# A hybrid RG-LRU / gMLP / conv-FFN block on one core: residual steps, one modulation and the last residual are moved

## The chip, the core and the metric

The kernel runs on one core of one Trainium2 chip. The metric is the device time of one execution in microseconds; the table below gives the median of three runs. One execution more was profiled: its trace is what the rows below are read from.

Engines are named as in the profile: PE (TensorE, matmuls), PEld (its weight loads), DVE (VectorE), ACT (ScalarE), POOL (GpSimd), SP (SyncE, which here only issues DMAs).

## The reference

One residual block, 2048 positions, width 1024, one batch element, all float32. What matters here:

```python
mod = silu(c) @ w_ada + b_ada                 # six vectors of 1024: sh_m, sc_m, gt_m, sh_f, sc_f, gt_f
h = rmsnorm(x, g_mix_pre) * (1 + sc_m) + sh_m
y = mixer(h @ w_in) @ w_out                   # RG-LRU heads and gMLP heads, each normed
x = x + gt_m * rmsnorm(y, g_mix_post)         # first residual
h = rmsnorm(x, g_ffn_pre) * (1 + sc_f) + sh_f
up = causal_conv3(h @ w_up)                   # 6144 columns: g_ff, v_ff
y = (gelu(g_ff) * v_ff) @ w_down              # 3072 -> 1024
x = x + gt_f * rmsnorm(y, g_ffn_post)         # last residual
```

## The kernel before, in words

Activations lie with the 1024 channels on partitions (8 blocks of 128) and positions along the free axis. Every matmul is done as three: each float32 operand is split into a high and a low part of the `fp32r` type (`split`, lines 136 and 141), and high x high, high x low and low x high are added in PSUM (`mm3`).

The mixer runs over four chunks of 512 positions (`c` = 0 to 3), the FFN over two chunks of 1024 (`C` = 0, 1). For each FFN chunk an *up* phase runs over 24 blocks of 128 gate and 128 value columns (`f`), and writes the gated product to `gd` in DRAM; then two *down* phases (`t` = 0, 1, 512 positions each) read it back. So the program is: mixer, up 0, down 00, down 01, up 1, down 10, down 11. In an up phase one block (`up_pair`) is seven products of 12 matmuls, 84 in all, made from seven weight pieces (`up_weights`), of which POOL computes four differences (lines 951 to 959), ACT and DVE the split.

Work beside the main line is written as Python generators that stand in a list `bg`; each `tick()` lets every generator go one step. `up_phase` has two ticks a block. Two such generators start at block `PLAIN + 1` = 3 of up 0:

- `late_chunks`: the first residual of mixer chunks 2 and 3, whose mixer outputs were kept in DRAM (`o2d`). One step of `late_post` (line 571 on) loads a tile of `x` and one of `o2d`, does two `scalar_tensor_tensor` (line 583), an add (line 584), a store to `x2d` (line 585), a square on ACT (line 215) and a sum of squares on POOL (line 219). Each chunk has four such steps, then a sum over partitions by two matmuls with a matrix of ones (line 199).
- `ada_task(5, 1)`: the sixth modulation vector, `gt_f`: eight loads of a weight tile and eight multiply-adds (lines 275 and 277), then eight PE transposes (line 284) and two reductions (line 285). The vectors 2, 3 and 4 are made the same way during the mixer (`ada_task(2, 2)`, `(3, 1)`, `(4, 1)`), where each half of the transposes has a PSUM tile of its own, out of four.

The loads of `x` and of the modulation's weights, and POOL's temporary `wt` of line 951, share one SBUF pool of three buffers (`lp`, tag `ld`).

A down phase ends with `evict`: for each of eight PSUM banks ACT squares (line 1074) and copies (line 1075); DVE adds the squares in pairs of blocks (line 1077) and folds the two halves (line 1101). `final()` then makes the norm (lines 199 to 203), scales each block (line 1112), adds a tile of `x2d` loaded into an `ld` buffer (lines 1109 and 1113) and stores the result (line 1114). For down 11 this stands at the end of the program.

The framework's scheduler sets the order of instructions on each engine from the order written, priorities and its own model of durations; an engine works through its queue in that order.

Of the kernel before, what the change touches and what calls it, by code (L numbers as in the profile page):

```python
# [15 lines left out]
P = 128  # L16
# [24 lines left out]
def block_kernel(ctx: ExitStack, tc: tile.TileContext, xt, cols, rows, wada, wada_r, win_k, win_s, win_v, wgate, wsp, wout, wup, wdown, out):  # L41
# [225 lines left out]
    def ada_task(m, pause=0):  # L267

        acc = tp.tile([P, 8, P], F32, tag="t4", name=f"ada_m{m}")
        flat = acc.rearrange("p k c -> p (k c)")  # L270
        for kt in range(8):
            w = lp.tile([P, 8 * P], F32, tag="ld", name=f"wada_{m}_{kt}")
            sync.dma_start(out=w, in_=wada_r[m - 2, kt])
            if kt == 0:
                vec.tensor_scalar(out=flat, in0=w, scalar1=cact[:, 0:1], scalar2=None, op0=ALU.mult)
            else:
                vec.scalar_tensor_tensor(out=flat, in0=w, scalar=cact[:, kt:kt + 1], in1=flat, op0=ALU.mult, op1=ALU.add)
            yield from wait(1 + pause)
        yield from wait(5)
        o = modv[:, m]  # L280
        for q in range(2):
            pt = bank(f"adaps_m{m}_{q}").rearrange("p (b c) -> p b c", c=P)
            for kb in range(4):
                pe.transpose(out=pt[:, kb], in_=acc[:, 4 * q + kb], identity=ident)
            vec.tensor_reduce(out=o[:, 4 * q:4 * q + 4], in_=pt, axis=mybir.AxisListType.X, op=ALU.add)
        vec.tensor_tensor(out=o, in0=o, in1=bav[:, m], op=ALU.add)
# [626 lines left out]
    def conv(C, blk, R):  # L913
# [3 lines left out]
        for t, s in ((1, 1), (0, 2)):  # L917
            vec.scalar_tensor_tensor(out=a[:, s:], in0=R[:, :FT - s], scalar=w[t], in1=a[:, s:], op0=ALU.mult, op1=ALU.add)  # L918
        if C == 0:
            vec.tensor_copy(out=ftails[:, blk], in_=R[:, FT - 2:FT])  # L920
        else:
            for t, s in ((1, 1), (0, 2)):
                vec.scalar_tensor_tensor(out=a[:, :s], in0=ftails[:, blk, 2 - s:], scalar=w[t], in1=a[:, :s], op0=ALU.mult, op1=ALU.add)  # L923
# [104 lines left out]
    def up_phase(C, f0, on=lambda f: None):  # L1028
        before = None
        for f in range(f0, NF):  # L1030
# [2 lines left out]
            next(g)  # L1033
            if before:
                drain(before)
            tick()
            next(g)
            before = g
            tick()
# [4 lines left out]
    def down(C, t):  # L1044
# [21 lines left out]
            mm3(pts[d], (wh[:, d], wl[:, d]), G[f], f == 0, f == NF - 1)  # L1066

        O, acc = [], []

        def evict(d):  # L1070
            if d % 2 == 0:
                acc.append(t4(f"fs{n}_{d}"))
                O.append(t4(f"fo{n}_{d}"))
            act.activation(out=acc[-1][:, d % 2], in_=pts[d], func=AF.Square)
            act.copy(out=O[-1][:, d % 2], in_=pts[d])
            if d % 2 and d > 1:
                vec.tensor_tensor(out=acc[0], in0=acc[0], in1=acc[-1], op=ALU.add)

        for f in range(2):
# [15 lines left out]
        for d in range(8):  # L1095
# [1 line left out]
                mm(f, d)  # L1097
            evict(d)
            tick()
        a = acc[0]  # L1100
        vec.tensor_tensor(out=a[:, 0], in0=a[:, 0], in1=a[:, 1], op=ALU.add)
        hl = rms_split(a[:, 0], f"fr{n}")

        def final():
            r = rms_bcast(hl, 1.0, f"fr{n}")
            yield
            for j in range(4):
                xr = lp.tile([P, 2, 512], F32, tag="ld", name=f"fx{n}_{j}")
                sync.dma_start(out=xr, in_=x2d[C, :, 2 * j:2 * j + 2, sl])
                for b in range(2):  # L1110
                    o = O[j][:, b]
                    vec.scalar_tensor_tensor(out=o, in0=o, scalar=gf[:, 2 * j + b:2 * j + b + 1], in1=r, op0=ALU.mult, op1=ALU.mult)
                vec.tensor_tensor(out=O[j], in0=O[j], in1=xr, op=ALU.add)
                sync.dma_start(out=out[C, :, 2 * j:2 * j + 2, sl], in_=O[j])
                yield
# [27 lines left out]
            tick()  # L1143
        up_plain(0, f)
    drain(*st)
    up_phase(0, PLAIN, lambda f: start(late_chunks(), ada_task(5, 1)) if f == PLAIN + 1 else None)
    drain()
    vec.tensor_tensor(out=gf, in0=modc[:, 40:48], in1=colr("g_ffn_post", 0, 8), op=ALU.mult)
    for t in range(2):
        start(h2_sums(1, t, from_x2(1, t), True))  # L1150
        down(0, t)
        drain()
    up_phase(1, 0, lambda f: [drain(done.pop(0)) for _ in done[:]] if f == 1 else None)
    for t in range(2):
        down(1, t)
# [72 lines left out]
```

## Time and profile before

| | us |
|---|---|
| median of 3 runs | 2222.09 |
| lowest, highest | 2219.21, 2222.97 |
| the profiled execution | 2222.2 |
| its span in the trace | 2220.4 |

| engine | busy us | share of the span |
|---|---|---|
| PE | 2072.0 | 93% |
| PEld | 1700.7 | 77% |
| DVE | 1435.9 | 65% |
| ACT | 928.8 | 42% |
| POOL | 424.8 | 19% |

Matmuls overlap, so a busy PE does not say at what pace it works. A stretch is better judged by the number of matmuls in it and by the granted clock (1.00 is the level of 2.4 GHz, 0.50 that of 1.2 GHz). In the trace, the mixer lies before 674 us, up 0 ends at about 1190, down 00 at 1324, down 01 at 1456, up 1 at 1924, the last matmul of down 11 starts at 2190.89, and the span ends at 2220.4.

### The profile page before, as it was taken

To read this page: it belongs to the slowest core of one execution; us is meant where nothing else is said; L and a number is where in the kernel's file an instruction comes from. 1 tells how busy PE (TensorE), PEld (TensorE's weight loads), DVE (VectorE), ACT (ScalarE), POOL (GpSimd) and SP (SyncE) were. 2 spreads that over 40 slices of the span, in tenths; PEclk is the share of its full clock that TensorE was granted. 3 is DMA by queue.
4 is the path that set the end of the run, shared out by engine and by line. 5 is a ranking of instruction groups with operands and counts; after the bars stand their busy time and mean duration, and the time that the engine had idled before them with its cause. 6 is when DMAs were issued, how large, how long until landed. Compare 5 with 4: busy or idle time off the path is not lost.

```text
span 2220.4 us, 24098 instructions
## 1 busy us (share of the span) xinstructions
PE 2072.0 (93%) x9032; PEld 1700.7 (77%) x9032; DVE 1435.9 (65%) x1598; ACT 928.8 (42%) x1154; POOL 424.8 (19%) x248
## 2 busy tenths in 40 slices
PE   5898969999998998799999999989999999999995
PEld 4686858888877876588888888868888888888883
DVE  7788789795766887898777437474444444533634
ACT  3472733534635544355555344343233332422422
POOL 4454243234203332443320000020000000000000
PEclk9999989999999999899999999999999999999997
DMA  8587568587674887877775546537666666444541
GB/s 315 187 311 286 193 242 291 206 287 256 225 268 164 305 314 265 311 264 276 271 291 189 181 134 215 173 120 286 220 221 224 220 223 221 145 159 149 212 148 60
DMA packets 157748, 501.14 MB, mean 226 GB/s; under 512 B 15296, under 2 KB 15424, under 8 KB 157632
## 3 DMA queue, kind: packets, MB, share of 16 engines
q1 hardware_dynamic: 149568, 470.25, 59.9%
q0 software_dynamic: 6912, 25.17, 2.9%
q10 hardware_dynamic: 1152, 4.19, 0.5%
q8 instruction: 71, 1.16, 0.2%
q14 instruction: 45, 0.37, 0.1%
HBM read 343.31 MB, written 156.24 MB: 225 GB/s over the span
## 4 chain that ended last, share of the span: by engine, by line
PE 73%; DVE 14%; ACT 4%; DMA 4%; issue 4%; POOL 1%; SPq 0%; DVEq 0%; ACTq 0%; POOLq 0%
PE dn L177 8%; PE dn L178 8%; PE dn L179 8%; PE upa L973 7%; PE upa L972 7%; PE upa L971 7%; PE upc L973 3%; PE upc L972 3%; PE upc L971 3%; PE upb L973 2%; PE upb L971 2%; PE upb L972 2%; PE lg L177 1%; PE lg L178 1%; PE lg L179 1%
## 5 line engine op out<-in xcount | busy, mean ns | idle before, releaser
L177 PE MATMUL dn<-gh,wd_h 128*128 128x512 f32 x768 | 297.0, 390 | 2.9 <-ACT fr_r L202 1.6
L178 PE MATMUL dn<-gl,wd_h 128*128 128x512 f32 x768 | 296.6, 389 | 0.0
L141 DVE TENSOR_TENSOR wd_l<-wd_r,wd_h 128x1024 fp32r<-128x1024 f32 x96 | 118.0, 1230 | 231.9 <-ACT wd_h L136 216.1
L179 PE MATMUL dn<-gh,wd_l 128*128 128x512 f32 x768 | 265.0, 389 | 0.0
L136 ACT CAST wd_h<-wd_r 128x1024 fp32r<-128x1024 f32 x96 | 101.2, 1056 | 286.8 <-PE dn L178 276.1
L918 DVE SCALAR_TENSOR_TENSOR a<-Rg,prm,a 128x1023 f32<-128x1023 f32 x92 | 132.4, 1439 | 126.9 <-ACT a L916 126.7
L177 PEld LDWEIGHTS dn<-gh,wd_h 128*128 128x128 f32 x768 | 144.2, 188 | 35.4 <-ACT wd_h L136 3.0
L179 PEld LDWEIGHTS dn<-gh,wd_l 128*128 128x128 f32 x768 | 144.1, 188 | 29.8
L178 PEld LDWEIGHTS dn<-gl,wd_h 128*128 128x128 f32 x768 | 144.2, 188 | 29.8
L918 DVE SCALAR_TENSOR_TENSOR a<-Rv,prm,a 128x1023 f32<-128x1023 f32 x92 | 121.9, 1325 | 38.7 <-ACT a L916 38.5
L951 POOL TENSOR_TENSOR wt<-wuv,wug 128x512 f32<-128x512 f32 x24 | 39.3, 1637 | 523.7 <-DMA wuv<-in_wup_dram 411.7
L916 ACT ACTIVATE a<-Rv,prm 128x1024 f32<-128x1024 f32 x46 | 57.2, 1244 | 133.3 <-DVE Rv L1020 132.6
L136 ACT CAST wt<-wt 128x512 fp32r<-128x512 f32 x72 | 44.7, 622 | 113.3 <-PE upa L973 39.5
L141 DVE TENSOR_TENSOR wt<-wt,wt 128x512 fp32r<-128x512 f32 x72 | 62.7, 873 | 24.0 <-ACT wt L136 23.8
L976 ACT ACTIVATE a<-a 128x1024 f32<-128x1024 f32 x48 | 50.9, 1061 | 53.7 <-DVE a L923 31.9
L1020 DVE TENSOR_TENSOR Rv<-upa,m 128x512 f32<-128x512 f32 x46 | 31.6, 687 | 58.3 <-PE upa L973 58.3
L141 DVE TENSOR_TENSOR gl<-gr,gh 128x1024 fp32r<-128x1024 f32 x48 | 58.5, 1218 | 12.5 <-PE upa L973 6.3
L977 DVE TENSOR_TENSOR a<-a,a 128x1024 f32<-128x1024 f32 x48 | 58.8, 1225 | 2.5 <-ACT a L976 2.5
L916 ACT ACTIVATE a<-Rg,prm 128x1024 f32<-128x1024 f32 x46 | 57.2, 1243 | 4.4 <-DVE a L918 3.2
L136 ACT CAST gh<-gr 128x1024 fp32r<-128x1024 f32 x48 | 50.8, 1058 | 13.3 <-DMA gr<-gd 6.1
L1024 ACT COPY Rg<-upa 128x512 f32<-128x512 f32 x46 | 26.8, 584 | 69.7 <-PE upa L973 69.7
L959 POOL TENSOR_TENSOR wt<-wug,wt 128x512 f32<-128x512 f32 x24 | 39.9, 1662 | 82.4 <-DVE wt L141 55.5
(583 smaller groups left out, 5738.5 us busy)
## 6 DMA issues: line engine op xcount, KB each, us to landing
wd_r<-in_wdown_dram SPq DMA_DIRECT2D x96, 512.0 KB, 4.4
wkd<-wt SPq DMA_DIRECT2D x88, 512.0 KB, 4.0
wkd<-w SPq DMA_DIRECT2D x66, 512.0 KB, 3.7
w<-wkd SPq DMA_DIRECT2D x66, 512.0 KB, 4.3
gd<-a SPq DMA_DIRECT2D x48, 512.0 KB, 3.9
gr<-gd SPq DMA_DIRECT2D x48, 512.0 KB, 3.5
wrt<-wkd SPq DMA_DIRECT2D x44, 512.0 KB, 4.3
wt<-wkd SPq DMA_DIRECT2D x44, 512.0 KB, 4.6
```

The costliest lines, as they stand in the source:

```text
L136: act.copy(out=hi, in_=src)
L141: (leng or vec).tensor_tensor(out=lo, in0=src, in1=hi.bitcast(F32), op=ALU.subtract)
L177: pe.matmul(out=out, lhsT=wh, rhs=mh, start=first, stop=False)
L178: pe.matmul(out=out, lhsT=wh, rhs=ml, start=False, stop=False)
L179: pe.matmul(out=out, lhsT=wl, rhs=mh, start=False, stop=last)
L916: act.activation(out=a, in_=R, func=AF.Identity, scale=w[2], bias=col("ffn_conv_b", blk))
L918: vec.scalar_tensor_tensor(out=a[:, s:], in0=R[:, :FT - s], scalar=w[t], in1=a[:, s:], op0=ALU.mult, op1=ALU.add)
L971: pe.matmul(out=pt, lhsT=wh, rhs=mh, start=first and not more and k == 0, stop=False, skip_group_check=more)
L972: pe.matmul(out=pt, lhsT=wh, rhs=ml, start=False, stop=False, skip_group_check=more)
L973: pe.matmul(out=pt, lhsT=wl, rhs=mh, start=False, stop=last and k == 3, skip_group_check=more)
L976: act.activation(out=g, in_=g, func=AF.Gelu_apprx_tanh)
L977: vec.tensor_tensor(out=g, in0=g, in1=v, op=ALU.mult)
```

## The change

- In `up_phase` one of the two ticks of a block is taken out, so a background generator goes one step a block.
- `ada_task(5, 1)` and the product `gf` made from it move from up 0 to down 00.
- In `ada_task`, the two halves of the transposes of the mixer's vectors share one PSUM tile.
- The two-column copy `ftails` of the conv (line 920) moves from DVE to ACT.
- In `evict`, each block's square gets a tile of its own and is added as one block of 512; the fold of line 1101 goes. In down 11 the copies of the odd blocks move from ACT to DVE.
- In down 11 the residual is copied from `x2d` to `out` by one DMA from DRAM to DRAM, and the four scaled tiles are added to it by accumulating DMAs that POOL issues; the loads of line 1109 and the adds of line 1113 go there.

```diff
@@ ada_task @@
         o = modv[:, m]
+        pts = [bank(f"adaps_m{m}_{q}") for q in range(2)] if banks else psum(f"adaps_m{m}").rearrange("p q c -> q p c")
         for q in range(2):
-            pt = bank(f"adaps_m{m}_{q}").rearrange("p (b c) -> p b c", c=P)
+            pt = pts[q].rearrange("p (b c) -> p b c", c=P)
@@ conv @@
-            vec.tensor_copy(out=ftails[:, blk], in_=R[:, FT - 2:FT])
+            act.copy(out=ftails[:, blk], in_=R[:, FT - 2:FT])
@@ up_phase @@
                 drain(before)
-            tick()
             next(g)
             before = g
             tick()
@@ down @@
+        end = C == NFC - 1 and t == 1
         def evict(d):
             if d % 2 == 0:
-                acc.append(t4(f"fs{n}_{d}"))
                 O.append(t4(f"fo{n}_{d}"))
-            act.activation(out=acc[-1][:, d % 2], in_=pts[d], func=AF.Square)
-            act.copy(out=O[-1][:, d % 2], in_=pts[d])
-            if d % 2 and d > 1:
+            acc.append(e_tile(f"fs{n}_{d}"))
+            act.activation(out=acc[-1], in_=pts[d], func=AF.Square)
+            o = O[-1][:, d % 2]
+            if end and d % 2:
+                vec.tensor_copy(out=o, in_=pts[d])
+            else:
+                act.copy(out=o, in_=pts[d])
+            if d:
                 vec.tensor_tensor(out=acc[0], in0=acc[0], in1=acc[-1], op=ALU.add)
...
-        a = acc[0]
-        vec.tensor_tensor(out=a[:, 0], in0=a[:, 0], in1=a[:, 1], op=ALU.add)
-        hl = rms_split(a[:, 0], f"fr{n}")
+        hl = rms_split(acc[0], f"fr{n}")
+        if end:
+            copied = sync.dma_start(out=out[C, :, :, sl], in_=x2d[C, :, :, sl])
@@ final @@
-                xr = lp.tile([P, 2, 512], F32, tag="ld", name=f"fx{n}_{j}")
-                sync.dma_start(out=xr, in_=x2d[C, :, 2 * j:2 * j + 2, sl])
+                if not end:
+                    xr = lp.tile([P, 2, 512], F32, tag="ld", name=f"fx{n}_{j}")
+                    sync.dma_start(out=xr, in_=x2d[C, :, 2 * j:2 * j + 2, sl])
...
+                if end:
+                    add = pool.dma_start(out=out[C, :, 2 * j:2 * j + 2, sl], in_=O[j], accum_op=ALU.add)
+                    tc.add_manual_dep(add.ins, copied.ins.name, mybir.DependencyInfo(mybir.DependencyClass.Sync, mybir.DependencyReason.DATA), reason="residual in place")
+                    continue
@@ main @@
-    up_phase(0, PLAIN, lambda f: start(late_chunks(), ada_task(5, 1)) if f == PLAIN + 1 else None)
+    up_phase(0, PLAIN, lambda f: start(late_chunks()) if f == PLAIN + 1 else None)
     drain()
-    vec.tensor_tensor(out=gf, in0=modc[:, 40:48], in1=colr("g_ffn_post", 0, 8), op=ALU.mult)
     for t in range(2):
-        start(h2_sums(1, t, from_x2(1, t), True))
+        start(h2_sums(1, t, from_x2(1, t), True), *(() if t else (ada_task(5, 1),)))
         down(0, t)
         drain()
+        if t == 0:
+            vec.tensor_tensor(out=gf, in0=modc[:, 40:48], in1=colr("g_ffn_post", 0, 8), op=ALU.mult)
```

What the scheduler makes of it, at three places. First, POOL's queue in up 0 before the change, from the weight differences of block 5 on; `rq2_s0` is the running sum of squares of mixer chunk 2, `wt0_5` the temporary of block 5:

```order
L959 TENSOR_TENSOR wt0_5_5552<-wug0_5_5548,wt0_5_5552 128x512
L219 TENSOR_TENSOR rq2_s0_5471<-rq2_s0_5471,rq2_s1_5545 128x1024
L951 TENSOR_TENSOR wt0_6_5726<-wuv0_6_5723,wug0_6_5722 128x512
...
L959 TENSOR_TENSOR wt0_6_5726<-wug0_6_5722,wt0_6_5726 128x512
L219 TENSOR_TENSOR rq2_s0_5471<-rq2_s0_5471,rq2_s2_5644 128x1024
L951 TENSOR_TENSOR wt0_7_5882<-wuv0_7_5879,wug0_7_5878 128x512
```

The same sums in POOL's queue after the change (line 951 has become 952, 959 has become 960):

```order
L960 TENSOR_TENSOR wt0_8_6000<-wug0_8_5996,wt0_8_6000 128x512
L219 TENSOR_TENSOR rq2_s0_5674<-rq2_s0_5674,rq2_s1_5833 128x1024
L952 TENSOR_TENSOR wt0_9_6160<-wuv0_9_6157,wug0_9_6156 128x512
L954 TENSOR_TENSOR wt0_9_6160<-wuv0_9_6157,wt0_9_6160 128x512
...
L960 TENSOR_TENSOR wt0_9_6160<-wug0_9_6156,wt0_9_6160 128x512
...
L219 TENSOR_TENSOR rq2_s0_5674<-rq2_s0_5674,rq2_s2_5993 128x1024
```

Before, a sum stood in front of the first difference of blocks 6, 7 and so on, in each block; now the first one stands in front of block 9, and the sums are further apart.

Second, PE in the mixer where vector 2 is transposed (`adaps_m2`), between two tiles of the output projection of chunk 0 (`o0_1`, `o0_2`), before:

```order
L179 MATMUL o0_1_2002<-rg0h1_1770,wout0_1_1_l_2061 128x512
L284 MATMUL adaps_m2_0_2092<-ident_87,ada_m2_637 128x128 x4
L284 MATMUL adaps_m2_1_2098<-ident_87,ada_m2_637 128x128 x4
L177 MATMUL o0_2_2120<-rl0h0_1576,wout0_2_0_h_2123 128x512
L178 MATMUL o0_2_2120<-rl0l0_1577,wout0_2_0_h_2123 128x512
```

And after:

```order
L179 MATMUL o0_1_2002<-rg0h1_1770,wout0_1_1_l_2061 128x512
L285 MATMUL adaps_m2_2092<-ident_87,ada_m2_637 128x128 x4
L177 MATMUL o0_2_2119<-rl0h0_1576,wout0_2_0_h_2122 128x512
...
L178 MATMUL o0_2_2119<-rg0l1_1771,wout0_2_0_h_2122 128x512
L285 MATMUL adaps_m2_2092<-ident_87,ada_m2_637 128x128 x4
L179 MATMUL o0_2_2119<-rg0h1_1770,wout0_2_0_l_2123 128x512
```

The second four transposes now stand 23 matmuls of `o0_2` later, and wait there for the reduction of the first four.

Third, DVE at the end of the program before: the sums of squares (`fs`), the norm (`fr`) and the scaled tiles (`fo`):

```order
L1077 TENSOR_TENSOR fs_0_15074<-fs_0_15074,fs_2_15092 128x1024
L1077 TENSOR_TENSOR fs_0_15074<-fs_0_15074,fs_4_15111 128x1024
L1077 TENSOR_TENSOR fs_0_15074<-fs_0_15074,fs_6_15130 128x1024
L1101 TENSOR_TENSOR fs_0_15074<-fs_0_15074 128x512
L140 CAST fr_hl<-fs_0_15074 128x512
```

And after, with the four copies of odd blocks among them:

```order
L1078 COPY fo_0_15092<-dn_1_14320 128x512
L1082 TENSOR_TENSOR fs_0_15093<-fs_0_15093,fs_1_15102 128x512
L1082 TENSOR_TENSOR fs_0_15093<-fs_0_15093,fs_2_15113 128x512
L1078 COPY fo_2_15112<-dn_3_14328 128x512
L1082 TENSOR_TENSOR fs_0_15093<-fs_0_15093,fs_3_15123 128x512
L1078 COPY fo_4_15133<-dn_5_14336 128x512
L1082 TENSOR_TENSOR fs_0_15093<-fs_0_15093,fs_4_15134 128x512
L1078 COPY fo_6_15154<-dn_7_14401 128x512
L1082 TENSOR_TENSOR fs_0_15093<-fs_0_15093,fs_5_15144 128x512
L1082 TENSOR_TENSOR fs_0_15093<-fs_0_15093,fs_6_15155 128x512
L1082 TENSOR_TENSOR fs_0_15093<-fs_0_15093,fs_7_15165 128x512
L140 CAST fr_hl<-fs_0_15093 128x512
```

Four instructions in front of the norm have become eleven, each over one block.

## Rows read from the trace of the kernel before

**Rows 1.** Windows: stretches in us, busy time and count by engine, clock.

```profile
core 0: us, PE busy (x) PEld busy (x) DVE busy (x) ACT busy (x) POOL busy (x), PEclk, DMA share, GB/s
750.00:800.00 50.00, 50.00 (x223) 41.33 (x222) 40.12 (x49) 26.47 (x36) 7.50 (x6) 1.00 0.84 299
800.00:950.00 150.00, 121.95 (x472) 95.48 (x471) 131.96 (x131) 66.16 (x93) 67.89 (x35) 0.91 0.76 284
950.00:1183.00 233.00, 233.00 (x1033) 192.93 (x1032) 185.84 (x218) 123.82 (x178) 63.79 (x44) 1.00 0.76 280
...
1455.00:1700.00 245.00, 234.28 (x1020) 192.23 (x1019) 127.14 (x168) 80.95 (x106) 9.55 (x4) 0.98 0.63 217
```

**Rows 2.** Waits of PE, 735 to 960 us: total us, times, longest.

```profile
PE upc L971 <- ACT wt L136: 6.0, 3, 3.3
PE rq_m L199 <- DVE rq_hl L140: 5.6, 2, 3.0
PE upc L971 <- ACT m L1008: 5.5, 1, 5.5
PE upc L973 <- DVE wt L141: 4.9, 2, 3.7
```

**Rows 3.** Waits of POOL, 735 to 960 us, same columns.

```profile
POOL rq_s L219 <- ACT rq_s L215: 30.3, 2, 23.2
POOL wt L951 <- DVE ol L584: 28.2, 1, 28.2
```

**Rows 4.** By tile: instructions of the residual and the modulation, ns min/median/max.

```profile
L583 DVE SCALAR_TENSOR_TENSOR ol<-ol,gm,rp_r x16: 737/747/1767, 779.9 to 922.1; 128x512 f32<-128x512 f32 x16
L584 DVE TENSOR_TENSOR ol<-ol,xr x8: 1208/1212/1224, 782.4 to 925.5; 128x1024 f32<-128x1024 f32 x8
...
L277 DVE SCALAR_TENSOR_TENSOR ada_m<-wada,cact,ada_m x28: 1180/1274/3408, 113.5 to 935.9; 128x1024 f32<-128x1024 f32 x28
```

**Rows 5.** Groups by line on DVE, 950 to 1183 us: the conv's copy.

```profile
L920 DVE COPY ftails<-Rg 128x2 f32<-128x2 f32 x13 | 7.6, 582 | 0.0
```

**Rows 6.** Timeline, mixer, around the transposes: start, length, engine; then idle before.

```profile
308.94 0.77 PE L177 MATMUL o<-rl0h,wout_h 128*128 128x512 f32 x1 [18.13 <-DVE modc L285]
...
299.76 8.44 DVE L257 SCALAR_TENSOR_TENSOR x2lo<-x,modc,x2hi 128x512 fp32r<-128x512 f32 x2
308.12 1.27 DVE L285 TENSOR_REDUCE modc<-adaps_m 128x4 f32<-128x512 f32 x2
...
300.68 2.36 POOL L219 TENSOR_TENSOR rl_s<-rl_s,rl_s 128x1024 f32<-128x1024 f32 x1
```

**Rows 7.** Waits at the start of up 1: of PE, and of POOL.

```profile
PE upc L971 <- ACT wt L136: 8.8, 1, 8.8
...
POOL wt L951 <- DVE fo L1113: 31.9, 1, 31.9
```

**Rows 8.** Timeline of ACT at the end: first and last of sixteen evictions.

```profile
2187.23 0.60 ACT L1074 ACTIVATE fs<-dn 128x512 f32<-128x512 f32 x1 [5.97 <-PE dn L179]
...
2194.40 0.77 ACT L1075 COPY fo<-dn 128x512 f32<-128x512 f32 x1
```

**Rows 9.** Timeline of DVE at the end.

```profile
2195.98 0.69 DVE L1101 TENSOR_TENSOR fs<-fs 128x512 f32<-128x512 f32 x1
...
2199.47 3.35 DVE L203 RECIPROCAL fr_r<-fr_r 128x512 f32<-128x512 f32 x1 [1.61 <-ACT fr_r L202]
2202.86 5.39 DVE L1112 SCALAR_TENSOR_TENSOR fo<-fo,gf,fr_r 128x512 f32<-128x512 f32 x8
...
2215.21 1.23 DVE L1113 TENSOR_TENSOR fo<-fo,fx 128x1024 f32<-128x1024 f32 x1 [3.56 <-DMA fx<-x2d]
```

**Rows 10.** DMA: rate in 40 slices of 2200 to 2221 us; POOL's plain stores.

```profile
GB/s 0 0 0 0 0 0 0 0 0 0 0 0 0 0 0 0 0 0 0 133 371 359 168 78 187 230 375 410 406 414 402 375 90 351 394 254 0 0 0 0
...
L169 POOL DMA_DIRECT2D kept_o<-wout_h x8: 531/572/717, 252.9 to 307.6; - x8
...
DMA to landing us min/median/max: 3.1/5.5/11.5
```

## The prediction, made before the changed kernel ran

> **What bounds the kernel now.** I read the page's share of busy time first: PE is busy for 93%, so only stretches in which PE loses pace can give anything. To find them I read windows: how many matmuls lie in a stretch, and how long it is. From 950 to 1183 us, up 0 without residual steps, 1033 matmuls take 233 us, with PE busy throughout and the clock at 1.00 [rows 1]: 0.2256 us each, the full pace. A block of 84 lasts 18.95 us. From 800 to 950 there are only 472, worth 106.5 us at that pace, so **43.5 us are lost**: 28.05 idle, and 15.45 by which the busy 121.95 exceeds 106.5, at a granted clock of 0.91. From 1455 to 1700 the 1020 matmuls are worth 230.1, and 14.9 us are lost.
>
> Next I ask who is late there. PE's waits from 735 to 960 name ACT and DVE as they split the weight pieces `wt`, ACT on `m`, and the sum of a chunk's squares, `rq_hl` [rows 2]. Behind them stands POOL: it waits up to 23.2 us for the residual's square before it can add it, with the next block's differences queued behind, and once 28.2 us for a buffer that the residual's add gives back [rows 3]. The residual steps run from 779.9 to 925.5 [rows 4], which is the slow stretch.
>
> Two more places belong to the change: one wait of 18.13 us in the mixer [rows 6], and the stretch from the last matmul (2190.89) to the span's end, 29.5 us.
>
> **The change part by part.** All sums start from the profiled execution, 2222.2 us, of which 2220.4 are span; that is 0.1 over the median, so it stands for the runs shown.
>
> *Up 0, one step a block.* DVE is busy 185.84 of 233 us without background [rows 1], 15.1 us a block. A residual step is two of line 583 at 0.747 and one of line 584 at 1.212, so 2.71; a modulation step is 1.27 [rows 4]. Before, while a chunk's four steps run, two of them and one of the modulation give 15.1 + 5.4 + 1.3 = 21.8 us a block, 2.85 more than PE needs; in the four blocks where they run that is 11.4 of the 28.05 us that PE stood idle. The rest I read as POOL's queue: in the order of instructions its first difference (line 951) of blocks 6, 9 and 10 stands only 9, 1 and 1 matmuls ahead of the first product that uses it, so whatever holds POOL then holds PE. After, a block has at most one step and no modulation; the copy of line 920 also goes to ACT (0.58 each, about one a block [rows 5]). That is 15.1 + 2.7 - 0.6 = 17.2, 1.7 us of slack. ACT takes the copy at 123.82 busy of 233 [rows 1]. The first differences now stand at least 61 matmuls ahead of their use, 61 x 0.2256 = 13.8 us, since the modulation's loads no longer share the buffers of `wt` here. So both causes go, and what isn't spread stays: the two sums over partitions, for which PE waited 5.6 us [rows 2]. I round that to 5 and take **-38.5**. Ends: -43.5 (nothing stays), and -22 (what DVE's overfill cost goes, with as much of the rest as gives half).
>
> *The modulation.* Down 00 takes eight loads, eight multiply-adds on DVE (8 x 1.27 = 10.2 us) and eight transposes. DVE is far from full in the down phases, and the multiply-adds stand beside some 130 us of matmuls. The new DRAM copy moves 2 MB in and 2 MB out, which the queues fit in during up 0; at the 414 GB/s seen at the end [rows 10] it takes about 10 us of transfer, beside 280 GB/s in use [rows 1]. It is issued by SP after the residual's last store, and weight loads queue behind it. Hidden by loads made ahead: 0; uncovered, half of it delays a block: +5. I take **+1**.
>
> *Transposes that share a tile.* PE waited 18.13 us, since `o0_2` had no PSUM tile until DVE had reduced `adaps_m2_0` (308.12), and DVE was held by the pair of line 257, 8.44 us long [rows 6]. After, `o0_2` has a tile and 23 matmuls go first, 23 x 0.2256 = 5.2 us; then the second transposes wait for the same reduction, at the same 308. So **-5.2**, and not -18 (ends -2, -7). For vectors 3 and 4 nothing waits at this place: 0.
>
> *Start of up 1.* PE waits 8.8 us for ACT's split, and POOL 31.9 us for the last use of a residual load in down 01's final [rows 7]. The change leaves this in place: the final is the same, only its norm starts some 1.2 us earlier by the folded addition that goes (0.69 [rows 9]) and shorter additions. **-1.2** (0 to -2).
>
> *End.* ACT made its sixteen evictions from 2187.23 to 2195.17 [rows 8], 0.5 each; with twelve left it is done near 2193.2. DVE has eleven instructions in front of the norm instead of four; at 0.69 for one block [rows 9] they are 7.6 us, from about 2188.5 to 2196.1, against 2196.67 before: -0.5. The norm then takes what it took, with a reciprocal of 3.35 [rows 9], and ends at 2202.3 instead of 2202.82. The eight scaled blocks took 5.39 [rows 9]: pairs at 2203.65, 2205.0, 2206.35, 2207.7. Before, three things came after: the adds, a wait of 3.56 us for the last residual tile [rows 9], and a store that ends 3.96 us after the last add (2216.44 to 2220.4). After, POOL issues four DMAs, 0.55 each by its plain stores [rows 10]. No row shows an accumulating DMA. If it costs what a plain store does, the end is 2207.7 + 0.55 + 3.96 = 2212.2: -8.2. If each byte goes twice, half a MB at 414 GB/s is 1.27 us, twice 2.53, four of them 10.1 from 2204.25, with the store's fixed 2.7 (3.96 - 1.27) behind: 2217.1, **-3.3**. If they go one after the other at the landing of POOL's stores, 5.5 us each [rows 10], 2226.3: +5.9; at the 11.5 of the slowest, +30. I take the second: the operand must be read, and nothing in the program puts one behind the other.
> The Trainium skill bears on this price. "Collectives: The Full Stack", section "The bandwidth ceiling: the fold count and why AG ≠ RS ≠ AR", says that an add made by a DMA reads two sources where a copy reads one, both on one ring, so that it runs at about half a copy's rate; no run here shows it yet. By it the end would be the second value, and by the plain store's rows alone the total would be 4.9 us lower.
>
> Sum: 2222.2 - 38.5 + 1 - 5.2 - 1.2 - 3.3 = **2175.0 us**.
>
> **The rivals.**
> 1. *DVE's steps get longer beside POOL.* Line 583 takes 0.737 to 1.767 us [rows 4], and the pair of line 257 took 8.44 while POOL added squares from 300.68 [rows 6]: such a meeting costs about 1.03 us. POOL's four differences stand in each block, so with three more meetings in a block with a step, DVE's 17.2 become 20.3, 1.35 over 18.95. In the slow stretch 28.05 idle became 43.5, a factor of 1.55; eight steps give 8 x 1.35 x 1.55 = 16.7, and the total is about **2192**. It decides from the second meeting a block. Against it: blocks without steps hold the same differences and run at full pace.
> The Trainium skill, "SBUF — State Buffer", section "Who interferes with whom", states it as a rule: a DVE instruction with two inputs in SBUF and a GpSimd instruction that reads SBUF exclude each other, and the later one stands still until the first is done. The spread of line 583 agrees. By it more than two meetings a block are likely, which is why this rival has a large chance.
> 2. *Slower: each sum holds POOL.* The residual's sum on POOL waits for DVE's add and ACT's square, and the next block's differences are queued behind it. The first of them held POOL for 23.2 us [rows 3]. Spread, each of the eight steps has its sum in front of some block's differences; if each held POOL for 23.2, the 13.8 us by which these lead are used up and PE waits 9.4 us, eight times: 75, which is 32 more than was lost, even at full clock. With the other terms, 2222.2 + 32 - 8.7 = about **2245**. The total is slower than before from (43.5 + 8.7) / 8 = 6.5 us a step on, so from 20 us of hold. Against it: the one other such wait was 7.1 (30.3 - 23.2), and from 750 to 800, where the first sum held POOL, 223 matmuls stand in 50 us at full clock [rows 1].
> 3. *The accumulating DMAs go one after the other.* The end costs +5.9 instead of -3.3: **2184**; at the slowest landing 2208.
> 4. *The spread brings nothing.* The waits behind ACT and the load buffers are moved and not removed; then only the small terms stay: 2222.2 - 8.7 = **2213**, or about the time before if the end also goes wrong.
>
> **How the numbers follow.** The forecast with its own range, 2163 to 2187 (the terms' ends of -43.5, -8.2, -7 and -2 can't all hold at once), has 0.62; rival 1, 2188 to 2203, 0.20; rival 3, 0.06; rival 4, 0.05, of which half ends within 0.2%; rival 2, 0.07. The range of 2163 to 2203 holds most of the first two and of the third. A measurement of this kernel tells about 0.2% (4.4 us) from no change. Faster than that: 0.62 + 0.20 + 0.06, and the better half of rival 4, so 0.90; the same 0.03; slower 0.07.
>
> **What would show it.** In up 0, from block 3 on, matmuls at 0.2256 us with the clock at 1.00 and no waits for `wt`; DVE near 17.2 of 18.95 us a block, and line 583 with a median near 0.75 (rival 1: above 1; rival 2: POOL held some 20 us by each sum, and PE waiting for `wt` after it). In the mixer a wait of about 13 us, now at the second transposes. At the start of up 1 a loss of 14 to 15 us as before. At the end, the norm's sums done some 0.5 us sooner, and the four DMAs overlapping, with the last landed some 9 us after the last scaled block. The forecast is wrong if POOL still waits for the residual's buffers in up 0, if down 00 shows a new wait of PE, or if the DMAs queue one behind the other.

## The result and the profile after

The changed kernel takes 2192.61 us (median of 4 runs, 2190.29 to 2193.87), against 2222.53 before (2219.21 to 2224.73): a ratio of 0.9865 with a 95% interval of 0.9848 to 0.9882, or 29.9 us less. The forecast was 2175.0 in a range of 2163 to 2203: inside the range, but 17.6 us short of the gain, and outside the part of the range, 2163 to 2187, that the forecast had for itself. One execution of the kernel before (7386 us) and one of the first combination below (5766 us) ran far longer than all others and stand in no range or ratio here (without it, the median of that combination would be 2167.2 us).

The profiled execution took 2193.9 us, its span 2192.1, which is 28.3 less than the span before. Cut at the first matmul of each phase, it goes like this (the last matmul is that of down 11's products):

| part | before, us | after, us | measured | forecast |
|---|---|---|---|---|
| start to the first matmul of up 0 | 681.87 | 684.84 | +3.0 | -5.2 |
| up 0 | 504.40 | 473.05 | -31.4 | -38.5 |
| down 00 and 01 | 269.63 | 270.17 | +0.5 | +1 |
| up 1 | 466.07 | 466.42 | +0.4 | -1.2 |
| down 10 and 11, to the last matmul | 268.93 | 268.92 | 0.0 | 0 |
| last matmul to the span's end | 29.5 | 28.7 | -0.8 | -3.3 |

Windows of the kernel after, to be laid beside [rows 1] (same columns; up 0 now ends at 1158, up 1 begins at 1428):

```profile
core 0: us, PE busy (x) PEld busy (x) DVE busy (x) ACT busy (x) POOL busy (x), PEclk, DMA share, GB/s
750.00:800.00 50.00, 50.00 (x222) 41.37 (x221) 40.59 (x40) 28.21 (x45) 14.57 (x9) 1.00 0.78 286
800.00:950.00 150.00, 146.32 (x638) 120.28 (x637) 129.91 (x132) 80.62 (x128) 62.53 (x34) 0.99 0.84 306
950.00:1157.00 207.00, 203.22 (x889) 167.43 (x888) 177.21 (x176) 111.88 (x180) 71.90 (x41) 0.99 0.83 304
1428.00:1672.00 244.00, 234.61 (x1015) 192.23 (x1014) 126.81 (x167) 79.98 (x104) 8.91 (x4) 0.97 0.65 218
```

From 800 to 950 us PE now makes 638 matmuls and not 472. At 0.2256 us each they are worth 143.9, so 6.1 us are lost there instead of 43.5; the residual steps now come one a block, four from 815 to 882 us and four from 954 to 1021, and the stretch after 950 loses 6.4. At the start of up 1 the 1015 matmuls are worth 229.0 of 244: 15.0 lost, as before.

Waits of PE from 735 to 960 us after the change, all that are listed [rows 2]:

```profile
PE upa L972 <- ACT x L1013: 2.2, 1, 2.2
PE upa L972 <- DVE Rv L1021: 1.5, 1, 1.5
```

The waits for `wt`, `m` and `rq_hl` are gone. POOL, which had waited 30.3 us for the residual's squares and 28.2 for a residual add [rows 3], now waits in that stretch only for loads of its weights, for DVE's split of `wt`, and once for a store:

```profile
POOL wt L952 <- DMA wuv<-in_wup_dram: 42.1, 4, 12.3
POOL wt L960 <- DVE wt L141: 40.7, 9, 13.9
POOL wt L952 <- DVE wt L141: 37.1, 5, 9.8
POOL wt L960 <- DMA wkd<-wt: 19.5, 1, 19.5
```

At the end, DVE's scaled blocks and POOL's accumulating DMAs, by the timeline, and then the rate of the DMAs in 40 slices of 2158 to 2194 us (0.9 us each):

```profile
2174.76 5.39 DVE L1118 SCALAR_TENSOR_TENSOR fo<-fo,gf,fr_r 128x512 f32<-128x512 f32 x8
2176.72 3.79 POOL L1120 DMA_DIRECT2D out_dram<-fo  x3 [709.18 <-DVE fo L1118]
2183.20 1.22 POOL L1120 DMA_DIRECT2D out_dram<-fo  x1 [2.69 <-issue]
```

```profile
GB/s 0 0 0 0 0 0 0 0 0 0 0 0 0 0 0 0 0 0 0 0 0 0 30 75 125 212 198 187 200 196 214 209 184 205 203 91 2 0 0 0
```

The four tiles, 2.1 MB, start slowly, with 30, 75 and 125 GB/s in the first three slices, and then drain at about 200 GB/s, half of what the loads and stores at the end reached before (375 to 414 [rows 10]). The last is done 12 us after DVE.

### The profile page after: what moved, and what is told of

It reads as the page before. It is cut to its first block, busy times and chain, and to the rows that moved or that the text cites. A ratio compares the mean times of both kernels' runs of the same rounds, so it can differ in the third digit from the quotient of the medians.

```text
span 2192.1 us, 24121 instructions
## 1 busy us (share of the span) xinstructions
PE 2065.3 (94%) x9032; PEld 1697.9 (77%) x9032; DVE 1427.9 (65%) x1562; ACT 928.2 (42%) x1198; POOL 438.6 (20%) x252
## 4 chain that ended last, share of the span: by engine, by line
PE 43%; issue 36%; DVE 12%; DMA 4%; ACT 3%; POOL 1%; SPq 0%; POOLq 0%; DVEq 0%; ACTq 0%
PE dn L177 4%; PE dn L178 4%; PE dn L179 4%; PE upa L972 3%; PE upa L974 3%; PE upa L973 3%; PE upc L972 2%; PE upc L974 2%; PE upc L973 1%; PE lg L177 1%; PE lg L178 1%; PE lg L179 1%; DVE acc L642 1%; PE v L424 1%; PE v L425 1%
## 5 line engine op out<-in xcount | busy, mean ns | idle before, releaser
L919 DVE SCALAR_TENSOR_TENSOR a<-Rv,prm,a 128x1023 f32<-128x1023 f32 x92 | 129.6, 1409 | 37.2 <-ACT a L917 36.8
L1120 POOL DMA_DIRECT2D out_dram<-fo x4 | 5.0, 1296 | 711.9 <-DVE fo L1118 709.2
L141 DVE TENSOR_TENSOR gl<-gr,gh 128x1024 fp32r<-128x1024 f32 x48 | 58.5, 1219 | 11.4 <-PE upa L974 6.3
L219 POOL TENSOR_TENSOR rp_s<-rp_s,rp_s 128x1024 f32<-128x1024 f32 x12 | 33.0, 2754 | 118.5 <-ACT rp_s L215 118.4
```

Source lines behind the costliest of these rows:

```text
L141: (leng or vec).tensor_tensor(out=lo, in0=src, in1=hi.bitcast(F32), op=ALU.subtract)
```

## The experiments

Each kernel below is the changed kernel with one edit, unless the text says otherwise. Where a phase's time is given, it is from the run's profile, cut as in the table above; times of whole kernels are medians, of four or five executions. The kernel before was timed again beside each group of runs, with medians of 2220.0 to 2222.8 us, so a difference of 2 or 3 us between kernels of different groups shows nothing.

**Two steps a block again.** In `up_phase`:

```diff
                 drain(before)
+            tick()
             next(g)
```

> The changed kernel with the second background step of a block put back in the up phases; the modulation stays in down 00. Theory (the spacing of the residual steps decides, because it sets how far ahead POOL's first weight difference of a block stands: here 24, 1 and 23 matmuls ahead of its use in blocks 6, 9 and 10, against 67 to 146 in the changed kernel): most of up 0's gain goes, the phase takes 490 to 505 us instead of 473, and the kernel 2210 to 2225 us. Rival (the modulation's loads and multiply-adds made the waits): 2190 to 2200 us.

Measured: 2213.05 us, up 0 494.7: 21.7 us of up 0's 31.4 are lost again. POOL and PE, 735 to 960 us:

```profile
POOL wt L952 <- DVE ol L585: 65.4, 4, 31.5
...
PE upc L972 <- ACT m L1009: 16.0, 3, 14.2
PE rq_m L199 <- DVE rq_hl L140: 7.0, 1, 7.0
```

The wait for a residual add before POOL's first difference is back, four times. So the spacing matters, as the theory had it; whether by DVE's load or by the buffers, this run doesn't tell.

**The sixth modulation in up 0 again**, still with one step a block:

```diff
-    up_phase(0, PLAIN, lambda f: start(late_chunks()) if f == PLAIN + 1 else None)
+    up_phase(0, PLAIN, lambda f: start(late_chunks(), ada_task(5, 1)) if f == PLAIN + 1 else None)
```

> The changed kernel with the sixth modulation vector made in up 0 again, beside the residual, one step a block. Theory (spacing decides): a few us only, since the first differences of a block still stand 15 to 64 matmuls ahead in the worst blocks (8, 14, 16); 2193 to 2203 us. Rival (the modulation's loads, which share POOL's buffers, made the waits): up 0 loses 20 us or more again, 2212 us or more.

Measured: 2202.90 us (2196.28 to 2206.56), up 0 and down 00 and 01 together 753.3 us instead of 743.2: +10.1, at the upper end of the theory's range. POOL waited for the modulation's multiply-adds to give buffers back, and PE for DVE:

```profile
POOL wt L952 <- DVE ada_m L277: 38.6, 3, 17.3
...
PE upa L972 <- DVE Rv L1021: 6.5, 3, 4.0
```

Together the two edits make 21.7 + 10.1 = 31.8 us; before the change up 0 and down 00 and 01 took 774.0, which is 30.8 more than after. So they explain the whole gain of up 0 and add up.

**Two steps a block with five load buffers.** The first of these kernels, with

```diff
-    tp = hp = ctx.enter_context(tc.tile_pool(name="tp", bufs=36))
+    tp = hp = ctx.enter_context(tc.tile_pool(name="tp", bufs=34))
...
-    lp = ctx.enter_context(tc.tile_pool(name="lp", bufs=3))
+    lp = ctx.enter_context(tc.tile_pool(name="lp", bufs=5))
```

> The kernel of the run with two steps a block (modulation in down 00), with five load buffers in place of three and 34 in place of 36 of the large temporaries. The residual's work on each engine is the same; POOL's first differences now stand at least 55 matmuls ahead of their use. In the run with three buffers POOL waited 65.4 us for residual adds that gave a buffer back, and up 0 took 494.7 us. Theory (the buffers, and with them the lead, make the waits): up 0 takes 472 to 481 us, the kernel 2190 to 2200 us. Rival (two steps overfill DVE, or PE waits behind queued copies and squares whatever the buffers): up 0 stays at 488 to 495 us, with PE's waits on `m` and `rq_hl` as before.

Measured: 2190.75 us, up 0 481.8, down from 494.7 and 0.8 over the theory's range; up 1, whose first difference also stands further ahead now, 452.0. The waits of POOL and PE, 735 to 960 us, and, by the timeline, ACT and DVE around the one long wait that stays:

```profile
POOL wt L952 <- DVE ol L585: 11.8, 2, 8.2
...
PE upc L972 <- ACT m L1009: 13.7, 3, 13.3
```

```profile
910.11 0.59 ACT L1009 COPY m<-upc 128x512 f32<-128x512 f32 x1 [5.09 <-DVE ol L584]
...
907.67 2.41 DVE L584 SCALAR_TENSOR_TENSOR ol<-ol,gm,rp_r 128x512 f32<-128x512 f32 x2
```

DVE does the same work and POOL the same sums, so 13.0 of the 21.7 us were the three buffers and not the load. What stays is mostly one wait, of 13.3 us, and a buffer has a part in it again. The copy `m` of block 10 takes over the buffer of `rp3_r`, in a pool of six: the program has it wait for the last instruction that reads `rp3_r`, line 584 of the last tile, which ends at 910.08, and the copy starts at 910.11. The kernel with three buffers shows the same wait (14.2), and the kernel before its shorter form (5.5 [rows 2]). DVE reaches that line late, after another step at 893 us and the block's own work, and shows no wait from 897.30 us on; so the wait is DVE's load as well as the shared buffer, and no run separates the two. With one step a block no copy `m` is listed as waiting for the residual.

**The conv's two-column copy on DVE again** (`vec.tensor_copy` for `act.copy`).

> The changed kernel with the two-column copy of the conv on DVE again. Theory (with one step a block DVE has slack, and the copy is under 0.6 us a block): 2191 to 2195 us, up 0 within 2 us of 473. Rival (DVE is at its limit in the blocks with steps): up 0 longer by 4 to 9 us, 2197 us or more.

Measured: 2194.83 us (2190.76 to 2196.18), up 0 472.9: no difference in up 0. Where DVE has slack the copy is free on either engine.

**A tile for each half of the transposes.** The line that makes `pts` goes, and each half takes a bank:

```diff
-            pt = pts[q].rearrange("p (b c) -> p b c", c=P)
+            pt = bank(f"adaps_m{m}_{q}").rearrange("p (b c) -> p b c", c=P)
```

> The changed kernel with a PSUM tile for each half of the mixer's transposes again. In the profile of the changed kernel the mixer's wait of 18.1 us became 13.2 us after 23 matmuls, but the mixer ended no sooner. Theory (the gain is used up at the mixer's end, where PE waits for ACT behind a load that comes back from DRAM): within 2 us of the changed kernel, 2190 to 2195 us, with a shorter wait ahead of the first up block. Rival (the gain is real and the mixer's end was late by chance in the one profile): 5 us slower, 2196 to 2200 us.

Measured: 2190.66 us (2189.17 to 2191.44), 2 us less than with the shared tile, whose executions overlap with these (2190.29 to 2193.87). The wait ahead of up 0 is 7.93 us here and 12.37 after the change (PE, by the timeline):

```profile
679.91 0.79 PE L971 MATMUL up<-h_00h,w 128*128 128x512 f32 x1 [7.93 <-ACT oo L559]
```

```profile
308.74 1.12 PE L285 MATMUL adaps_m<-ident,ada_m 128*128 128x128 f32 x4 [13.04 <-DVE modc L286]
...
461.62 0.66 PE L199 MATMUL rl_m<-rl_hl,onesD 128*128 128x512 f32 x1 [2.02 <-DVE rl_hl L141]
...
593.46 0.47 PE L199 MATMUL rg_m<-rg_hl,onesD 128*128 128x512 f32 x1 [2.56 <-DVE rg_hl L140]
...
684.84 0.80 PE L972 MATMUL up<-h_00h,w 128*128 128x512 f32 x1 [12.37 <-ACT oo L560]
```

```profile
673.63 0.39 PE L179 MATMUL o<-rg3h,wout_l 128*128 128x512 f32 x1
681.87 0.80 PE L971 MATMUL up<-h_00h,w 128*128 128x512 f32 x1 [7.85 <-ACT oo L559]
```

The first fence is the kernel with two tiles, the second the changed kernel, the third the kernel before, with the last matmul of the mixer and the first of up 0. PE does gain 5.1 us at 295 us (18.13 [rows 6] became 13.04), and pays at the norms of the next two chunks and at the mixer's end. Laid matmul by matmul beside the kernel before, the changed kernel is 5.7 us ahead after the transposes, 4.2 after the norm of the next chunk and 0.6 after the one behind it. Its last matmul of the mixer starts at 672.08 us, 1.6 ahead, and its first of up 0 is 3.0 behind. The two waits at the norms, of 2.0 and 2.6 us, stand in all eight kernels with the changed kernel's order of PE's instructions in the mixer, and are 0.4 and 0.9 us in the three with the order before; and PE waits 9.5 to 14.2 us ahead of up 0 in those eight, 6.8 to 7.9 in these three. At the mixer's end the order of SP's queue differs as well. In the last stage of the output projection, with two tiles:

```
L228 DMA xf_1_4581<-x2d 128x2x512
L562 DMA o2d<-oo_0_4547 128x1024
L164 DMA wout_3_0_h<-kept_o_0_2216 128x1024
```

and with the shared tile:

```
L164 DMA wout_3_0_l<-kept_o_1_2216 128x1024
L563 DMA o2d<-oo_0_4544 128x1024
L228 DMA xf_1_4578<-x2d 128x2x512
```

The load of `xf`, from which the input of up 0 is built, now stands behind a store that waits for PE's output: it was issued at 647.09 us, against 640.29 with two tiles. What is built from it is stored, and loaded again shifted (`hs`); ACT's casts of `hs` stand ahead of the eviction that PE waits for. That this order makes the longer wait is argued and not shown: no run changes it alone, and with it as in the changed kernel the wait was 9.46 us in the run with the mixed end below.

**Transposes written later.** For vector 2, the pause ahead of the transposes is made longer, so that both halves stand about 100 matmuls further down PE's queue:

```diff
-        yield from wait(5)
+        yield from wait(9 if m == 2 else 5)
```

> The changed kernel with the transposes of vector 2 written four background steps later, so that they stand some 100 matmuls further down PE's queue, beyond the reduction that PE waits 13 us for at 295 us. Theory (time that PE gains there is given back, since the norms at the chunks' ends and the loads at the mixer's end arrive no sooner): the wait at 295 goes, others at 459, 590 and 672 grow, and the first matmul of up 0 comes within 4 us of 683, the kernel 2188 to 2195 us. Rival (PE's wait was on the path): the mixer ends 10 to 13 us sooner, the kernel near 2181 us.

Measured: 2195.45 us, 0.5 over the theory's range, first matmul of up 0 at 686.6. PE, 290 to 330 us, every wait, and DVE just before:

```profile
313.84 0.76 PE L199 MATMUL rl_m<-rl_hl,onesD 128*128 128x512 f32 x1 [11.70 <-DVE rl_hl L140]
315.61 0.80 PE L199 MATMUL rl_m<-rl_hl,onesD 128*128 128x512 f32 x1 [1.01 <-DVE rl_hl L141]
317.23 0.77 PE L199 MATMUL rg_m<-rg_hl,onesD 128*128 128x512 f32 x1 [0.83 <-ACT rl_r L202]
...
300.84 8.44 DVE L257 SCALAR_TENSOR_TENSOR x2lo<-x,modc,x2hi 128x512 fp32r<-128x512 f32 x2
```

With the transposes out of the way PE runs on to the next thing, the sum over partitions, and waits 11.70 us there for the same engine, behind the same pair of line 257 (8.44 us, as in [rows 6]). So the wait at 295 us was DVE's backlog; the transposes were only the first instruction to meet it. The theory put the loss at later places, and it came at once.

**The last residual added by DVE again**, with the tiles loaded as before, and the rest of the end as changed.

> The changed kernel with the last residual as before: tiles loaded into SBUF, added by DVE, stored by SP; the squares stay summed block by block. Theory (the accumulating DMAs move each byte twice and give next to nothing): the stretch from the last matmul to the end is 28.5 to 29.5 us instead of 28.7, the kernel 2191 to 2195 us. Rival (they were worth the 3 us of the forecast's term): 2195 to 2197 us.

Measured: 2192.62 us, last matmul to the span's end 28.8 us, against 28.7 with the accumulating DMAs. They bring nothing.

**Plain stores in place of the accumulating DMAs.**

```diff
-                    add = pool.dma_start(out=out[C, :, 2 * j:2 * j + 2, sl], in_=O[j], accum_op=ALU.add)
+                    pool.dma_start(out=out[C, :, 2 * j:2 * j + 2, sl], in_=O[j])
```

> The changed kernel with plain stores by POOL in place of the accumulating DMAs, and without the copy of the residual: the last quarter of the output lacks the residual. In the changed kernel the 2 MB of the accumulating DMAs drain at about 200 GB/s for 10.4 us. Theory (an adding DMA moves at half the rate): plain stores run at about 400 GB/s, DVE's last scaled pair sets the end, and the stretch from the last matmul to the end falls from 28.7 to 23 to 24.5 us, the kernel to about 2187 us. Rival (POOL's issue, 1.22 us each with a wait of 2.7 ahead of the fourth, sets the end): 27 us or more of stretch, 2191 us or more.

Measured: 2186.09 us (2180.04 to 2189.36), and 22.3 us from the last matmul to the end. The last two of POOL's issues, and the rate in 40 slices of 2158 to 2188 us:

```profile
2180.96 0.72 POOL L1118 DMA_DIRECT2D out_dram<-fo  x1 [0.57 <-DVE fo L1116]
2182.46 0.72 POOL L1118 DMA_DIRECT2D out_dram<-fo  x1 [0.78 <-DVE fo L1116]
```

```profile
GB/s 0 0 0 0 0 0 0 0 0 0 0 0 0 0 0 0 0 0 0 0 0 0 0 0 0 0 0 0 0 300 388 300 371 328 371 333 382 22 0 0
```

300 to 388 GB/s instead of 200; the adding costs 28.7 - 22.3 = 6.4 us for four tiles, and POOL's issue takes 0.72 us instead of 1.22.

**One tile by an accumulating DMA, three by DVE.** Only two columns of blocks are copied ahead, and

```diff
-                if not end:
+                if not end or j:
...
-                if end:
+                if end and not j:
```

> The changed kernel with only the first of the four last tiles added by an accumulating DMA; the other three are loaded ahead into the three load buffers, added by DVE and stored by SP. Theory (the adding DMA's half rate sets the end of the changed kernel, the fourth load set it before): DVE ends 8 scaled blocks and 3 adds about 20.5 us after the last matmul, the store 4 us later: 24.5 us instead of 28.7, 2188 to 2189 us. Rival (loads or the adding DMA keep the stores late): 27 us or more, 2191 us or more.

Measured: 2183.55 us (2182.93 to 2185.58), 24.7 us from the last matmul to the end, as forecast. DVE's and SP's last rows, and the DMAs from 2146 us on, first their rate in 40 slices, then the packets of SP's three stores and of POOL's adding DMA:

```profile
2173.15 3.49 DVE L1123 TENSOR_TENSOR fo<-fo,fx 128x1024 f32<-128x1024 f32 x3
...
2174.39 2.64 SPq L1124 DMA_DIRECT2D out_dram<-fo  x3
```

```profile
GB/s 0 0 0 0 0 0 0 0 0 0 0 0 0 0 0 0 0 0 0 0 0 0 0 0 0 0 0 0 46 84 177 207 223 378 380 389 380 66 0 0
...
q1 hardware_dynamic: 816, 1.57, 11.7%
q0 software_dynamic: 272, 0.52, 10.5%
```

A rival for the half rate is the size of the packets: the four accumulating DMAs took 1088 for their 2.10 MB, and POOL's plain stores 576. But SP's plain stores here go in packets as small as the adding DMA's (816 for three tiles, 272 for one) and reach 378 to 389 GB/s, so the size isn't the cause.

No add waits for its load any more (3.56 us before [rows 9]), and the slow adding of one tile lies beside DVE's work. The kernel gained 9 us and not 4; in the profile 2.1 more lie in up 0 and 5.2 ahead of it, and I can put neither down to the edit. That only a quarter of the residual is copied in DRAM during up 0 doesn't explain the 2.1: the run with plain stores, which copies none, took 473.9 us there.

**All four residuals by accumulating DMAs.** The conditions on `end` in `down` and `final` go.

> The changed kernel with the residual of all four down phases copied in DRAM and added by accumulating DMAs; no final loads a tile into the buffers that POOL's differences use. Theory (up 1 loses its 16.6 us because POOL's first difference of block 1 waits for such a buffer and stands 1 matmul ahead of its use; here it stands 94 ahead): up 1 takes 452 to 457 us instead of 466, the kernel 2178 to 2185 us. Rival (POOL's queue now waits for DVE's scaled tiles, which holds the differences as long; or the adding DMAs slow the loads): up 1 within 3 us of 466, or longer.

Measured: 2181.53 us, up 1 452.0 instead of 466.4. At the start of up 1 in the changed kernel POOL waited as before [rows 7], and here no longer for an add:

```profile
POOL wt L952 <- DVE fo L1123: 29.4, 1, 29.4
```

```profile
POOL out_dram L1120 <- DVE fo L1118: 11.2, 1, 11.2
...
POOL out_dram L1120 <- DVE a L924: 2.4, 1, 2.4
```

The first fence is the changed kernel, 1420 to 1480 us, the second this one, 1405 to 1475. PE has no listed wait in that stretch here. But down 00 and 01 take 276.8 us instead of 270.2, with a new wait while down 00's tiles are added (PE, 1300 to 1345):

```profile
PE dn L177 <- ACT wd_h L136: 4.1, 2, 3.9
```

**Two combinations.** Both have two tiles for the transposes and the mixed end. The first adds down 01's residual by accumulating DMAs and leaves 00 and 10 alone:

> The changed kernel with a PSUM tile for each half of the transposes, the residual of down 01 added by accumulating DMAs, and at the end only the first tile added that way, the others by DVE from tiles loaded ahead. If the parts add up as measured alone (up 1 -14.4, end -4.0, transposes -2): 2192.6 - 20.4 = 2172 us; 2169 to 2176. If the adding DMAs of down 01 disturb up 1 when down 00's are not there, 2180 or more.

The second leaves 00, 01 and 10 alone and has five load buffers:

> As the run before in this row, but down 01's residual stays with loads and DVE, and there are five load buffers in place of three (34 large temporaries in place of 36), which puts POOL's first difference of up 1's block 1 51 matmuls ahead of its use. If a lead of 51 matmuls, 11.5 us, is enough: up 1 takes 452 to 457 us, up 0 a few us less than 473, the kernel 2168 to 2175 us. If not: up 1 stays above 460 us, the kernel 2178 us or more.

Measured: 2167.97 us, a ratio to the kernel before of 0.9759 (0.9745 to 0.9772), and 2168.81 us, 0.9773 (0.9759 to 0.9786). Up 1 takes 452.0 in both, down 00 and 01 270.2 and 267.9. So a lead of 51 matmuls suffices, and the new wait of the run before this pair came with the adding of down 00's tiles. Measured against the kernel before as timed beside them (2220.01 us), both beat the changed kernel by over 20 us.

## Why the prediction was right, and where it was not

The measured 2192.61 us lies in the stated range only through the part that rival 1 added to it, while more than half of what the forecast missed lies in terms that rival 1 doesn't touch. That the range holds is in good part luck.

- **Up 0: right in mechanism, 7 us too large.** Both causes that the text named, two steps on DVE and shared buffers of `wt`, were weighed, and the runs put 13.0 of the 21.7 us that the spacing is worth on the buffers; for the modulation's 10.1 POOL's wait of 38.6 us points the same way, but no run separates it. The step that gave 11.4 us to DVE's overfill is borne out only in part: with two residual steps a block and five buffers most of the loss goes, and what stays is mostly a wait in which DVE's lateness meets a third cause that the text missed, the pool of six that `rp3_r` shares with `m`. How two steps and the modulation together fare with five buffers, no run shows. The load of a block with a step was put too low. The two stretches with a step in each block, and one without any, hold

```profile
811.00:887.00 76.00, 72.32 (x314) 59.20 (x313) 68.79 (x62) 37.90 (x62) 40.95 (x21) 0.99 0.82 305
950.00:1026.00 76.00, 72.22 (x316) 59.15 (x315) 69.52 (x63) 38.52 (x64) 36.50 (x20) 0.99 0.87 311
1030.00:1150.00 120.00, 120.00 (x531) 99.32 (x530) 100.21 (x106) 67.87 (x109) 35.40 (x21) 1.00 0.83 311
```

  (columns as in [rows 1]). DVE is busy 68.79 us for 314 matmuls, 18.4 us a block of 84, and 18.5 in the second stretch, where 17.2 was forecast and PE needs 18.95. Without a step it is 15.9, part of which is the work for the second FFN chunk's input.
- **What stayed in up 0** was put at 5 us, for the two sums over partitions. These waits vanished (no `rq_m` in the list), but 12.5 us are lost between 800 and 1157. At 0.2256 us a matmul, 5.2 and 4.7 of them lie in the two stretches with a step in each block, where PE stands in four short waits for ACT's copy `x` and DVE's `Rv`, 7.5 us in all. Around the wait at 883 us ACT stands 6.96 us for a residual add before its square, with the copy behind, while the scaling pair takes 3.33 us on DVE beside POOL, and not twice 0.746:

```profile
881.97 1.06 ACT L215 ACTIVATE rq_s<-ol 128x1024 f32<-128x1024 f32 x1 [6.96 <-DVE ol L585]
...
877.35 3.33 DVE L584 SCALAR_TENSOR_TENSOR ol<-ol,gm,rp_r 128x512 f32<-128x512 f32 x2 [1.61 <-DMA ol<-o2d]
```

The Trainium skill, "SBUF — State Buffer", section "Who interferes with whom", states that a DVE instruction with two inputs in SBUF and a GpSimd instruction that reads SBUF exclude each other. The trace agrees here, with POOL in its differences from 877.14 to 880.1.

- **Rival 1** named 2192, the time that came, and is at most a part of the reason for it. The residual's own meetings with POOL have neither become more frequent nor longer: line 584 has nearly the minimum, median and maximum of [rows 4] (735/746/1777 ns), and 4 of its 16 instructions took over 1 us, where before 6 did. But the conv's line 919, which lies in every block, is longer where the steps are, first 811 to 887 us, then 1030 to 1150, then its longest instruction and POOL's sum of the residual's squares beside it:

```profile
L919 DVE SCALAR_TENSOR_TENSOR a<-Rv,prm,a x8: 1269/1806/2314, 810.4 to 873.9; 128x1023 f32<-128x1023 f32 x4, 128x1022 f32<-128x1022 f32 x4
...
L919 DVE SCALAR_TENSOR_TENSOR a<-Rv,prm,a x14: 1270/1283/2308, 1035.0 to 1149.7; 128x1023 f32<-128x1023 f32 x7, 128x1022 f32<-128x1022 f32 x7
...
884.19 3.10 DVE L919 SCALAR_TENSOR_TENSOR a<-Rg,prm,a 128x1023 f32<-128x1023 f32 x1 [1.65 <-ACT a L917]
...
883.84 2.36 POOL L219 TENSOR_TENSOR rq_s<-rq_s,rq_s 128x1024 f32<-128x1024 f32 x1
```

  That is the rival's mechanism at a line that it didn't name, about one meeting a block (18.4 against 17.2 us), and a block stayed under 18.95 us of DVE on the average of each stretch. Of the 18.9 us by which the profiled execution missed the forecast's gain, up 0 gives 7.1, of which the meetings can be a part, how large no run shows; the stretch ahead of it gives 8.2, the end 2.5, up 1 1.6, and the modulation takes 0.5 off.
- **The transposes: the step that failed.** -5.2 was forecast and +3.0 came. The wait fell to 13.04 us as the text had it; what failed is the step from a shorter wait to a shorter mixer. The text took a wait of 18.13 us and asked what stands ahead of it, not what PE needs next. With the wait cut by 5.1 us, PE loses the lead again at the norms of the next two chunks, where it waits for DVE, and ahead of up 0 (12.37 us for 7.85). With the transposes out of the way altogether it meets DVE's backlog at the chunk's own norm, as the run with later transposes shows with its 11.70 us. That the shared tile also reorders SP's loads at the mixer's end was to be seen in the order of instructions. How much it costs stays open within some us: in one profiled execution each, the eight kernels with the same order of PE's instructions in the mixer reached up 0 at 679.0 to 686.9 us, the three with the order before at 676.6 to 681.9. So the lost gain is shown, and the 3.0 us on top of it are within that spread.
- **Start of up 1:** nothing changed there, as forecast (a loss of 15 us). The earlier norm, for which -1.2 was taken, gave nothing.
- **The end: right in rate, short in overhead.** The sums finished 0.7 us sooner relative to the last matmul (0.5 forecast). The half rate came, but only after three slices at 30, 75 and 125 GB/s, so that the four tiles took some 12 us to drain and not 10.1. POOL's issue took 1.22 us and not 0.55; its stand of 2.69 us before the fourth cost nothing, since the rate stayed at 184 to 214 meanwhile. The last landing came 12 us after the last scaled block instead of 9.4, which is the 2.5 us missing.
The Trainium skill, "Collectives: The Full Stack", section "The bandwidth ceiling: the fold count and why AG ≠ RS ≠ AR", has the add that DMAs make in a ring of cores run at half a copy's rate, since it reads two sources. The traces agree in the rate, with about 200 against 300 to 388 GB/s, though no ring is at work here.
- **The modulation:** +0.5 for +1. Down 00 hides its multiply-adds.
- **Rivals 2 to 4:** no sum held POOL (no such wait in its list), the adding DMAs overlap, and up 0 became 31 us shorter.

## What to carry to other kernels

Count, in the order of instructions, how far ahead of its first use an in-order producer stands, and ask which pool its output comes from: here three buffers shared by unrelated loads made most of the waits (13.0 of 21.7 us), more than the work on DVE. With two steps a block, two more buffers took the kernel from 2213.05 to 2190.75 us, as far as spreading the steps did (2192.61). Before a wait of PE is counted as a gain, look at what PE needs next; if it comes from the same backlog, the wait only moves. And where an adding DMA replaces loads and adds, its half rate is paid in full at the end of a program, so here it paid to give it the tile that is ready first and nothing else.

## What the runs showed of the hardware

Four accumulating DMAs of half a MB from SBUF to DRAM drained at about 200 GB/s, after three slices at 30 to 125, and POOL took 1.22 to 1.28 us to issue one; plain stores of the same tiles drained at 300 to 388 and took 0.72 to 0.81 each. Two instructions of line 584 took 1.40 us alone and 3.33 to 3.47 where POOL was adding. Kernels with the same order of PE's instructions in the mixer differed there by up to 8 us, in one profiled execution each; why is open.
